# Choosing experts for both token tiles at once, both tiles' transposes ahead of the logits, and three forget-gate matmuls five steps later

## The chip, the core and the metric

The kernel runs on one core of a Trainium2 chip. The metric is the device time of one execution in microseconds. PE is the matrix engine, PEld its weight loads, DVE the vector engine, ACT the scalar engine, POOL GpSimd, and SP the engine whose queue issues nearly all loads of weights. A term used throughout: an engine takes its own instructions in the order in which they stand in its queue, so an instruction that waits holds up those behind it.

## What is computed

A decoder trunk of two layers on 256 tokens of width 1024, all in float32. Layer 0 mixes with a state-space scan (S5). Then one shared set of keys, values and forget gates is made, and layer 1 mixes with attention that reads it. Each layer ends in a mixture of 32 experts: a router picks one group of 8 experts out of 4 by the largest group logit, then the two best experts of that group. Cut to the two places that matter here:

```
def shared_kv(x, ...):                  # after layer 0
    k, v, fz = split(h @ kv_w)          # fz: (256, 16)
    logf = log_sigmoid(fz + kv_fb)
    fcum = cumsum(logf, over tokens)    # enters the attention logits of layer 1

def hier_moe(h, ...):                   # in both layers
    g_logits = t @ wg + bg              # (256, 4)
    g_top_v, g_idx = top_k(g_logits, 1)
    e_logits = (t @ we + be).reshape(-1, 4, 8)
    e_sel = e_logits at group g_idx
    top_v, top_i = top_k(e_sel, 2)
    w = softmax(top_v) * softmax(g_logits) at g_idx
    out = sum over the chosen experts of  w * (silu(t @ w1) * (t @ w3)) @ w2
```

## The kernel before

Tokens lie on the 128 partitions, as two tiles (i = 0, 1). All weights stream from HBM in blocks of 1 MB into a ring of 12 slots, to which the expert stages add some (`grow`). SP issues the loads in program order (`fetch`, L71), and a load waits until the work that last read its slot is done. So the stream runs at full rate while slots come free fast enough, and stands still while they don't.

**Order of work.** A scheduler places the instructions of ACT, DVE and POOL by its own model of time. Two stretches are written by hand: the start of each layer's experts (`start`, L571) on all engines, and PE's order alone from the keys and values to the end of the attention layer (`in_order`).

**The experts.** `start` finishes the last half of the residual stream `h`, transposes it on PE (`across`, L328; result copied to `hT` by ACT for tile 0 and by DVE for tile 1), forms the logits with 4 small matmuls for each tile and half (`logits`, L358), and takes the root mean square on DVE and POOL (`norm`, L341, result `rstds`). `step(fill, 4)` then puts 16 matmuls of a later gate on PE (L188). They read four weight blocks of the ring, which is how those four slots come free; ahead of them POOL clears a tile `rows` (L183) and SP loads two small bias rows into it (L185). Next come the choice of experts (`route_tile`, DVE alone), five small matmuls that count tokens per expert (`weigh`, L398), the placing matrix (`place`, L430), the gathering of tokens (`gather`, L441: PE, then ACT and DVE) and the first expert weights (`first`, L479), whose matmuls (L486) free the next slots. The loads of expert weights are put on SP's queue by `load`, at the end of `start` in program order.

`route_tile` is a generator for one tile. The two are run in lockstep, so that DVE gets step 1 of tile 0, step 1 of tile 1, step 2 of tile 0, and so on: 16 steps, 32 instructions, each step working on at most 36 columns.

**Keys, values and forget gates.** `project` (L1156) multiplies by a 512-column half of a weight matrix in eight steps ("quarters" of a block). For each quarter ACT and DVE split the weights into two parts (`split_next`, L1104 and L1105, three buffers `ws`), and PE does six matmuls of 512 columns (L1162). After each quarter, `tick` (L1117) advances a list of side jobs by one step. One of them is `forget_gates` (L1199): matmuls, a transpose, then a long chain of small DVE instructions for log-sigmoid that ends in `f_z` (L1239), then three small matmuls that sum over tokens:

```
V.scalar_tensor_tensor(fz, fp, -2.0, fz, op0=OP.mult, op1=OP.add)     # L1239
yield
pc = mm_tile()
PE.matmul(pc[:, 0:16], tri, fz[:, 0:16], start=True, stop=True)       # L1242
```

and two DVE copies of the sums (L1245, L1246). The job starts while the second half of the keys is projected and ends after the second quarter of the values (`project(hk, 0, use_v)`, L1409).

Of the kernel before, what the change touches and what calls it, by code (L numbers as in the profile page):

```python
# [15 lines left out]
OP = mybir.AluOpType  # L16
AX = mybir.AxisListType.X
# [5 lines left out]
NE = 32  # L23
# [4 lines left out]
BIG = 1e30  # L28
# [11 lines left out]
def trunk(ctx: ExitStack, tc: tile.TileContext, A, out, ring=12, ring2=4, ring3=5, ring4=3, ring5=4, lpb=2, TK=2):  # L40
    nc = tc.nc
    V, S, G, PE = nc.vector, nc.scalar, nc.gpsimd, nc.tensor
# [15 lines left out]
    def mm_tile():  # L58
        return psum.tile([128, 512], F32, tag="mm", name="mm", bufs=4)
# [56 lines left out]
    desc = const.tile([128, NE], F32, name="desc")  # L116
# [108 lines left out]
    def square(ssq, i, n):  # L225
        S.activation(mm_tile(), h[:, i, 512 * n:512 * n + 512], AF.Square, accum_out=ssq[:, i, n:n + 1])
# [85 lines left out]
    def moe(l, sh, g, gbc, c36, slots_):  # L312
# [13 lines left out]
        rstd = ma.tile([128, 2], F32, name="rstds")  # L326
# [25 lines left out]
        gm, gs, m1, m2, top, e2, r1, w1 = (t2(n, 1) for n in ("gm", "gs", "m1", "m2", "top", "e2", "r1", "w1"))  # L352
# [3 lines left out]
        pls = []  # L356

        def logits(i, n):  # L358
            if not pls:
                pls.append(acc_tile())  # L360
            for k in range(4 * n, 4 * n + 4):
                PE.matmul(pls[0][:, 64 * i:64 * i + 36], hTs[i][:, k, :], sw[:, k],
                          start=k == 0 and i == 0, stop=k == KD - 1, skip_group_check=True)

        def route_tile(pl, i):

            V.scalar_tensor_tensor(lg[:, i], pl[:, 64 * i:64 * i + 36], rstd[:, i:i + 1], c36, op0=OP.mult, op1=OP.add)
            yield
            gl = lg[:, i, 0:4]

            def rank_first(x, w, mx):

                V.tensor_reduce(mx[:, i], x, axis=AX, op=OP.max)
                yield
                V.scalar_tensor_tensor(cand[:, i, 0:w], x, mx[:, i], desc[:, NE - w:], op0=OP.is_equal, op1=OP.mult)
                yield
                V.tensor_reduce(top[:, i], cand[:, i, 0:w], axis=AX, op=OP.max)
                yield

            yield from rank_first(gl, 4, gm)  # L380
            V.tensor_scalar(gc[:, i], cand[:, i, 0:4], top[:, i], -BIG, op0=OP.is_lt, op1=OP.mult)
            yield
            V.tensor_tensor(ml[:, i].rearrange("p (a b) -> p a b", b=8),
                            lg[:, i, 4:36].rearrange("p (a b) -> p a b", b=8),
                            gc[:, i, :, None].to_broadcast([128, 4, 8]), op=OP.add)
            yield
            yield from rank_first(ml[:, i], NE, m1)
            V.tensor_scalar(o1[:, i], cand[:, i], top[:, i], None, op0=OP.is_equal)
            yield
            V.scalar_tensor_tensor(ml2[:, i], o1[:, i], -BIG, ml[:, i], op0=OP.mult, op1=OP.add)  # L390
            yield
            yield from rank_first(ml2[:, i], NE, m2)
            V.tensor_scalar(o2[:, i], cand[:, i], top[:, i], None, op0=OP.is_equal)
            yield
            V.tensor_tensor(selb[:, i], o1[:, i], o2[:, i], op=OP.add)
            yield

        def weigh():  # L398

# [171 lines left out]
        def start(gated, ssq, fill, after):  # L571

            with tc.manual_schedule(engines=ENGINES):
                steps = [gated(i) for i in range(2)]
                for st in steps:
                    next(st)
                for i, st in enumerate(steps):
                    next(st)
                    across(i, 1)
                    square(ssq, i, 1)  # L580
                    logits(i, 1)
                after()
                mb.append(es.enter_context(tc.tile_pool(name=f"moeb{l}", bufs=1, side="right")))
                norm(ssq)
                step(fill, 4)
                for _ in zip(*[route_tile(pls[0], i) for i in range(2)]):
                    pass
                mosti = weigh()
                place(0)
                gather(0)  # L590
                gate_values()
            load(l)
            return mosti
# [605 lines left out]
    def forget_gates():  # L1199


        pz = mm_tile()
        for kh in range(2):
            for a in range(2):
                for q in range(4):
                    k = 4 * kh + q
                    PE.matmul(pz[32 * q:32 * q + 32, :T], smallw[:, k, 0:32], hk[:, k, a, :].bitcast(F32),
                              start=kh + a == 0, stop=kh + a == 2)
        z4 = tp.tile([128, T], F32, tag="xf", name="z4", bufs=2)
        S.activation(z4, pz[:, :T], AF.Copy)  # L1210
        yield
        pt = mm_tile()
        for i in range(2):
            PE.transpose(pt[:, 128 * i:128 * i + 128], z4[:, 128 * i:128 * i + 128], ident)

        def a32(n):
            return ap.tile(t32, F32, name="f_" + n)

        fz, fa, fe, fs, f2, fp = (a32(n) for n in ("z", "a", "e", "s", "2", "p"))
        V.tensor_reduce(fz.rearrange("p (i e) -> p i e", i=2),  # L1220
                        pt[:, :T].rearrange("p (i q e) -> p i e q", i=2, q=4)[:, :, 0:16, :], axis=AX, op=OP.add)
        V.tensor_tensor(fz, fz, cols[:, C_FBR:C_FBR + 32], op=OP.add)
        V.tensor_scalar(fa, fz, -1.0, None, op0=OP.mult)
        V.tensor_tensor(fa, fa, fz, op=OP.min)
        yield
        p, two = exp_parts(ap, fa, t32)
        yield
        V.tensor_tensor(fe, p, two, op=OP.add)
        V.tensor_scalar(fs, fe, 2.0, None, op0=OP.add)
        V.reciprocal(fs, fs)  # L1230
        V.tensor_tensor(fs, fs, fe, op=OP.mult)
        V.tensor_tensor(f2, fs, fs, op=OP.mult)
        V.tensor_scalar(fp, f2, 1.0 / 15, None, op0=OP.mult)
        yield
        for c in (13, 11, 9, 7, 5, 3):
            V.scalar_tensor_tensor(fp, fp, 1.0 / c, f2, op0=OP.add, op1=OP.mult)
        V.scalar_tensor_tensor(fp, fp, 1.0, fs, op0=OP.add, op1=OP.mult)
        V.tensor_scalar(fz, fz, 0.0, None, op0=OP.min)
        V.scalar_tensor_tensor(fz, fp, -2.0, fz, op0=OP.mult, op1=OP.add)  # L1239
        yield  # L1240
        pc = mm_tile()
        PE.matmul(pc[:, 0:16], tri, fz[:, 0:16], start=True, stop=True)  # L1242
        PE.matmul(pc[:, 16:32], ones, fz[:, 0:16], start=True, stop=False)
        PE.matmul(pc[:, 16:32], tri, fz[:, 16:32], start=False, stop=True)
        V.tensor_copy(qn[:, :, :, 65], pc[:, :32].rearrange("p (i a) -> p i a", i=2))  # L1245
        V.tensor_scalar(kn[:, :, :, 64], pc[:, :32].rearrange("p (i a) -> p i a", i=2), -1.0, None, op0=OP.mult)  # L1246
# [335 lines left out]
```

## Time and profile before

| what | value |
|---|---|
| median of 3 runs | 818.82 us (817.67 to 820.29) |
| the profiled execution | 819.66 us, of which the span from the first to the last instruction is 817.9 us |
| mean granted clock of PE | 0.945 of full speed |
| PE / DVE / ACT / POOL busy | 86% / 47% / 28% / 6% of the span |
| moved from and to HBM | 299.30 MB, mean 366 GB/s over the span |

A busy share is an average over stages with different limits: in both layers' experts the DMA engines run at about 425 GB/s and set the pace; between them PE does. A row "idle before <- releaser" gives the idle time of that engine just before the instruction and what ended it. The granted clock is 1.00 at 2.4 GHz and 0.50 at 1.2 GHz.

### The profile page before, as it was taken

The numbers are of one execution on the slowest core, as the hardware profiler recorded it, in microseconds if no ns is written. First come the engines' busy times: TensorE is split into PE (matmuls) and PEld (weight loads), VectorE is DVE, ScalarE is ACT, GpSimd is POOL, SyncE is SP. The second block draws the span as 40 slices with busy tenths as digits, with TensorE's granted clock in tenths as the row PEclk, the third lists the DMA queues.
The fourth block names the chain that finished last, engine by engine and source line by source line (L and its number), as shares of the span: only waits on it lengthen the run. The fifth ranks groups of instructions, "written<-read, shape, count | busy, mean of one in ns | idle before, by whom it ended". The sixth has DMA issues, their size and how long they took to land. (4 is left out here: it accounts for less than half of the span.)

```text
span 817.9 us, 13668 instructions
## 1 busy us (share of the span) xinstructions
PE 706.3 (86%) x5510; PEld 402.8 (49%) x5510; DVE 381.3 (47%) x1025; ACT 232.1 (28%) x537; POOL 46.7 (6%) x52
## 2 busy tenths in 40 slices
PE   2797999898899998786779899999988999986776
PEld 0674776575533533131157567888764333331311
DVE  7685999774322332111165655775554222221202
ACT  4423333162201110000043265878722101100100
POOL 2000000000000000000001101570000000000000
PEclk9899999998999999789679999999999999999888
DMA  9998946777999999999999857592989999999996
GB/s 368 426 425 347 406 150 250 292 314 277 426 426 426 426 425 425 428 423 427 424 424 426 315 197 312 204 370 98 349 347 415 426 428 424 427 427 427 425 426 260
DMA packets 41828, 299.30 MB, mean 366 GB/s; under 512 B 4632, under 2 KB 4760, under 8 KB 5664
## 3 DMA queue, kind: packets, MB, share of 16 engines
q1 hardware_dynamic: 41344, 297.14, 88.3%
q10 hardware_dynamic: 416, 1.23, 0.4%
q8 instruction: 45, 0.74, 0.3%
q14 instruction: 23, 0.19, 0.1%
HBM read 297.31 MB, written 1.05 MB: 365 GB/s over the span
## 5 line engine op out<-in xcount | busy, mean ns | idle before, releaser
L486 PE MATMUL mm<-w,xg 128*32 128x512 f32 x1024 | 141.4, 637 | 24.0 <-DMA w<-wa 10.7
L486 PEld LDWEIGHTS mm<-w,xg 128*32 128x32 f32 x1024 | 29.6, 111 | 110.6 <-issue 62.8
L458 ACT ACTIVATE xg<-mm,sh,g 128x128 f32<-128x128 f32 x64 | 29.3, 457 | 181.0 <-PE mm L450 164.8
L1105 DVE TENSOR_TENSOR ws<-w,ws 128x512 fp32r<-128x512 f32 x80 | 58.2, 733 | 40.4 <-ACT ws L1104 40.1
L501 PE MATMUL mm<-w,aT 128*32 128x512 f32 x512 | 68.3, 655 | 9.2 <-DMA w<-wb 3.6
L450 PE MATMUL mm<-Pr,h 128*128 128x128 f32 x512 | 65.3, 281 | 11.2 <-DVE Pr L438 11.2
L1162 PE MATMUL acc<-ws,hn 128*128 128x512 f32 x288 | 73.9, 415 | 0.6 <-ACT hn L1140 0.6
L450 PEld LDWEIGHTS mm<-Pr,h 128*128 128x128 f32 x512 | 60.9, 194 | 26.6 <-issue 19.0
L508 PE MATMUL acc<-y,Sc 128*128 128x512 f32 x128 | 64.7, 629 | 6.5 <-DVE y L504 6.5
L1104 ACT ACTIVATE ws<-w 128x512 fp32r<-128x512 f32 x80 | 49.9, 629 | 54.5 <-PE acc L1162 43.6
L1162 PEld LDWEIGHTS acc<-ws,hn 128*128 128x128 f32 x288 | 56.0, 197 | 16.7 <-ACT hn L1140 1.9
L456 DVE TENSOR_SCALAR xg<-mm,g,sh 128x128 f32<-128x128 f32 x64 | 26.2, 410 | 74.1 <-ACT xg L458 74.1
L504 DVE TENSOR_TENSOR y<-mm,gbc 128x512 f32<-128x512 f32 x32 | 22.1, 692 | 64.7 <-PE mm L501 64.5
L491 ACT ACTIVATE a<-mm 128x256 f32<-128x256 f32 x16 | 6.1, 383 | 161.2 <-PE mm L486 161.2
L469 DVE COPY Sc<-mm 128x256 f32<-128x256 f32 x16 | 6.8, 425 | 83.8 <-PE mm L467 83.8
L508 PEld LDWEIGHTS acc<-y,Sc 128*128 128x128 f32 x128 | 22.2, 193 | 45.6 <-issue 26.8
L492 DVE TENSOR_TENSOR a<-a,mm 128x256 f32<-128x256 f32 x16 | 6.7, 419 | 75.0 <-ACT a L491 75.0
L501 PEld LDWEIGHTS mm<-w,aT 128*32 128x32 f32 x512 | 14.4, 114 | 50.6 <-issue 34.4
L785 PE MATMUL mm<-hnT,w 128*64 128x128 f32 x512 | 33.1, 289 | 2.7 <-ACT hnT L255 2.7
L961 PE MATMUL acc<-w,uT 128*128 128x512 f32 x64 | 30.5, 621 | 5.6 <-ACT uT L950 5.5
L785 PEld LDWEIGHTS mm<-hnT,w 128*64 128x64 f32 x512 | 31.3, 143 | 4.4 <-ACT hnT L255 3.7
L173 PE MATMUL mm<-w,sc 128*32 128x256 f32 x512 | 29.2, 380 | 0.0
(327 smaller groups left out, 951.8 us busy)
## 6 DMA issues: line engine op xcount, KB each, us to landing
w<-wa SPq DMA_DIRECT2D x128, 1024.0 KB, 19.5
w<-wb SPq DMA_DIRECT2D x64, 1024.0 KB, 19.7
w<-ada SPq DMA_DIRECT2D x36, 1024.0 KB, 10.6
w<-ada00s SPq DMA_DIRECT2D x8, 1024.0 KB, 18.1
w<-kvada SPq DMA_DIRECT2D x8, 1024.0 KB, 9.0
w<-win SPq DMA_DIRECT2D x4, 1024.0 KB, 14.9
w<-ada00g SPq DMA_DIRECT2D x4, 1024.0 KB, 18.8
w<-woutv SPq DMA_DIRECT2D x4, 1024.0 KB, 17.2
```

The lines of the kernel that those rows point to most:

```text
L173: PE.matmul(ps[32 * q:32 * q + 32, 0:256], sc32(2 * b + kk), bands(w[:, 1024 * kk:1024 * kk + 1024])[:, q], start=b + kk == 0, stop=b == 3 ...
L450: PE.matmul(px[:, 128 * c4:128 * c4 + 128], h[:, i, 128 * c:128 * c + 128], Pr[:, i].rearrange("p a b -> p (a b)"), start=i == 0, stop=i == 1)
L456: V.tensor_scalar(xg[:, c], src, g[:, c:c + 1], sh[:, c:c + 1], op0=OP.mult, op1=OP.add)
L458: S.activation(xg[:, c], src, AF.Identity, bias=sh[:, c:c + 1], scale=g[:, c:c + 1])
L486: PE.matmul(ph[32 * s:32 * s + 32, :], xg[:, k, 32 * s:32 * s + 32], w[:, 512 * s:512 * s + 512], start=k == 0, stop=k == KD - 1)
L501: PE.matmul(py[32 * s:32 * s + 32, :], aT[:, 128 * f + 32 * s:128 * f + 32 * s + 32], w[:, 512 * s:512 * s + 512], start=f == 0, stop=f == 1)
L508: PE.matmul(acc[i][n], scs[q][:, 128 * i:128 * i + 128], y[:, 512 * n:512 * n + 512], start=q == 0, stop=q == NQ - 1, skip_group_check=True)
L785: PE.matmul(ps[64 * v:64 * v + 64, 128 * hh:128 * hh + 128], w[:, k, c0:c0 + 64], hnT[:, k, v::2], start=k == 0 and hh == 0, stop=k == KD ...
L961: PE.matmul(val[t][n], uT[:, m, 128 * t:128 * t + 128], wval[m // 2][:, c0:c0 + 512], start=m == 0, stop=m == 7)
L1104: S.activation(o[:, 0], w, AF.Copy)
L1105: V.tensor_tensor(o[:, 1], w, o[:, 0].bitcast(F32), op=OP.subtract)
L1162: PE.matmul(pk[i], src[:, k, a, 128 * i:128 * i + 128], w[:, b], start=k + a + b == 0, stop=k == KD - 1 and b == 1)
```

## The change

Three edits.

1. In `start`, the transposes of both tiles are put on PE before the logits of either.
2. `route` takes the place of the two `route_tile` generators: one chain of instructions that work on both tiles side by side (up to 64 columns). What was one instruction with a scalar per token ("equal to the maximum, times rank") becomes two tensor instructions with a broadcast operand. 32 instructions become 21; only the logits and the masking of groups are still done for each tile.
3. `forget_gates` lets five more steps of `tick` go by before it asks PE for the three sums.

```diff
@@ -362,38 +362,32 @@
                 PE.matmul(pls[0][:, 64 * i:64 * i + 36], hTs[i][:, k, :], sw[:, k],
                           start=k == 0 and i == 0, stop=k == KD - 1, skip_group_check=True)
 
-        def route_tile(pl, i):
-
-            V.scalar_tensor_tensor(lg[:, i], pl[:, 64 * i:64 * i + 36], rstd[:, i:i + 1], c36, op0=OP.mult, op1=OP.add)
-            yield
-            gl = lg[:, i, 0:4]
+        def route(pl):
+
+            for i in range(2):
+                V.scalar_tensor_tensor(lg[:, i], pl[:, 64 * i:64 * i + 36], rstd[:, i:i + 1], c36,
+                                       op0=OP.mult, op1=OP.add)
 
             def rank_first(x, w, mx):
 
-                V.tensor_reduce(mx[:, i], x, axis=AX, op=OP.max)
-                yield
-                V.scalar_tensor_tensor(cand[:, i, 0:w], x, mx[:, i], desc[:, NE - w:], op0=OP.is_equal, op1=OP.mult)
-                yield
-                V.tensor_reduce(top[:, i], cand[:, i, 0:w], axis=AX, op=OP.max)
-                yield
-
-            yield from rank_first(gl, 4, gm)
-            V.tensor_scalar(gc[:, i], cand[:, i, 0:4], top[:, i], -BIG, op0=OP.is_lt, op1=OP.mult)
-            yield
-            V.tensor_tensor(ml[:, i].rearrange("p (a b) -> p a b", b=8),
-                            lg[:, i, 4:36].rearrange("p (a b) -> p a b", b=8),
-                            gc[:, i, :, None].to_broadcast([128, 4, 8]), op=OP.add)
-            yield
-            yield from rank_first(ml[:, i], NE, m1)
-            V.tensor_scalar(o1[:, i], cand[:, i], top[:, i], None, op0=OP.is_equal)
-            yield
-            V.scalar_tensor_tensor(ml2[:, i], o1[:, i], -BIG, ml[:, i], op0=OP.mult, op1=OP.add)
-            yield
-            yield from rank_first(ml2[:, i], NE, m2)
-            V.tensor_scalar(o2[:, i], cand[:, i], top[:, i], None, op0=OP.is_equal)
-            yield
-            V.tensor_tensor(selb[:, i], o1[:, i], o2[:, i], op=OP.add)
-            yield
+                V.tensor_reduce(mx[:, :, 0], x, axis=AX, op=OP.max)
+                V.tensor_tensor(cand[:, :, 0:w], x, mx.to_broadcast([128, 2, w]), op=OP.is_equal)
+                V.tensor_tensor(cand[:, :, 0:w], cand[:, :, 0:w],
+                                desc[:, None, NE - w:].to_broadcast([128, 2, w]), op=OP.mult)
+                V.tensor_reduce(top[:, :, 0], cand[:, :, 0:w], axis=AX, op=OP.max)
+
+            rank_first(lg[:, :, 0:4], 4, gm)
+            V.tensor_tensor(gc, cand[:, :, 0:4], top.to_broadcast([128, 2, 4]), op=OP.is_lt)
+            for i in range(2):
+                V.scalar_tensor_tensor(ml[:, i].rearrange("p (a b) -> p a b", b=8),
+                                       gc[:, i, :, None].to_broadcast([128, 4, 8]), -BIG,
+                                       lg[:, i, 4:36].rearrange("p (a b) -> p a b", b=8), op0=OP.mult, op1=OP.add)
+            rank_first(ml, NE, m1)
+            V.tensor_tensor(o1, cand, top.to_broadcast([128, 2, NE]), op=OP.is_equal)
+            V.scalar_tensor_tensor(ml2, o1, -BIG, ml, op0=OP.mult, op1=OP.add)
+            rank_first(ml2, NE, m2)
+            V.tensor_tensor(o2, cand, top.to_broadcast([128, 2, NE]), op=OP.is_equal)
+            V.tensor_tensor(selb, o1, o2, op=OP.add)
 
         def weigh():
 
@@ -578,13 +572,13 @@
                     next(st)
                     across(i, 1)
                     square(ssq, i, 1)
+                for i in range(2):
                     logits(i, 1)
                 after()
                 mb.append(es.enter_context(tc.tile_pool(name=f"moeb{l}", bufs=1, side="right")))
                 norm(ssq)
                 step(fill, 4)
-                for _ in zip(*[route_tile(pls[0], i) for i in range(2)]):
-                    pass
+                route(pls[0])
                 mosti = weigh()
                 place(0)
                 gather(0)
@@ -1238,6 +1232,8 @@
         V.tensor_scalar(fz, fz, 0.0, None, op0=OP.min)
         V.scalar_tensor_tensor(fz, fp, -2.0, fz, op0=OP.mult, op1=OP.add)
         yield
+        for _ in range(5):
+            yield
         pc = mm_tile()
         PE.matmul(pc[:, 0:16], tri, fz[:, 0:16], start=True, stop=True)
         PE.matmul(pc[:, 16:32], ones, fz[:, 0:16], start=True, stop=False)
```

Where instructions stand on the engines, before and after. Line numbers after the change are lower by 6 in `start` and by 4 or 6 further down.

PE at the forget gates. L1162 (L1156 after) are the projections of keys and values, six matmuls to a quarter; the rows with `f_z` are the three sums; L173 is a modulation matmul; L1129 the transposes for the queries. Before:

```order
L173 MATMUL mm<-w,sc 32x256 x32
L1162 MATMUL acc<-ws,hn 128x512 x12
L1242 MATMUL mm<-f_z,tri 128x16
L1243 MATMUL mm<-f_z,ones 128x16
L1244 MATMUL mm<-f_z,tri 128x16
L1162 MATMUL acc<-ws,hn 128x512 x84
```

After:

```order
L173 MATMUL mm<-w,sc 32x256 x32
L1156 MATMUL acc<-ws,hn 128x512 x42
L1238 MATMUL mm<-f_z,tri 128x16
L1239 MATMUL mm<-f_z,ones 128x16
L1240 MATMUL mm<-f_z,tri 128x16
L1156 MATMUL acc<-ws,hn 128x512 x54
```

The three sums now stand behind 42 projection matmuls instead of 12: seven quarters instead of two, out of the same 96.

DVE at the same place. `ws` is the DVE half of splitting one quarter of weights; `f_s`, `f_p` and `f_z` belong to the forget gates' chain, and L1245 and L1246 copy the sums out. Before:

```order
L1231 TENSOR_TENSOR f_s<-f_s,f_e 128x32
L1232 TENSOR_TENSOR f_3782<-f_s 128x32
L1233 TENSOR_SCALAR f_p<-f_3782 128x32
L1236 SCALAR_TENSOR_TENSOR f_p<-f_p,f_3782 128x32 x6
L1237 SCALAR_TENSOR_TENSOR f_p<-f_p,f_s 128x32
L1239 SCALAR_TENSOR_TENSOR f_z<-f_p,f_z 128x32
L1245 COPY qn<-mm 128x32
L1246 TENSOR_SCALAR kn<-mm 128x32
L1105 TENSOR_TENSOR ws<-w,ws 128x512 x14
```

After:

```order
L1225 TENSOR_TENSOR f_s<-f_s,f_e 128x32
L1226 TENSOR_TENSOR f_3771<-f_s 128x32
L1227 TENSOR_SCALAR f_p<-f_3771 128x32
L1099 TENSOR_TENSOR ws<-w,ws 128x512
L1230 SCALAR_TENSOR_TENSOR f_p<-f_p,f_3771 128x32 x3
L1099 TENSOR_TENSOR ws<-w,ws 128x512
L1230 SCALAR_TENSOR_TENSOR f_p<-f_p,f_3771 128x32 x3
L1099 TENSOR_TENSOR ws<-w,ws 128x512
L1231 SCALAR_TENSOR_TENSOR f_p<-f_p,f_s 128x32
L1233 SCALAR_TENSOR_TENSOR f_z<-f_p,f_z 128x32
L1099 TENSOR_TENSOR ws<-w,ws 128x512
L1241 COPY qn<-mm 128x32
```

Four quarters of weights are now split between the chain's steps and ahead of the copies that wait for PE; before, the chain and the copies stood in one piece. On ACT, POOL and SP nothing stands elsewhere.

PE at the start of layer 1's experts. L333 are transposes (4 for a tile and half), L362 logits (4 for a tile and half), L1399 (L1395 after) the last output projection, L188 the gate's matmuls. Before:

```order
L1399 MATMUL acc<-ws,oT 128x512 x4
L333 MATMUL mm<-ident,h 128x128 x8
L362 MATMUL acc<-smallw,hT 128x36 x12
L333 MATMUL mm<-ident,h 128x128 x4
L362 MATMUL acc<-smallw,hT 128x36 x4
L188 MATMUL acc<-w,sc 32x512 x16
```

After:

```order
L1395 MATMUL acc<-ws,oT 128x512 x4
L333 MATMUL mm<-ident,h 128x128 x8
L362 MATMUL acc<-smallw,hT 128x36 x4
L333 MATMUL mm<-ident,h 128x128 x4
L362 MATMUL acc<-smallw,hT 128x36 x12
L188 MATMUL acc<-w,sc 32x512 x16
```

The last transposes, those of tile 1, move from behind 12 logit matmuls to behind 4, and the last logits follow the others without a transpose in between. In layer 0 the same edit turns transposes, logits, transposes, logits (4 each) into 8 transposes and 8 logits.

## Rows read from the trace of the kernel before

**Rows 1.** The page: GB/s moved in 40 equal slices of 20.4 us.
```profile
GB/s 368 426 425 347 406 150 250 292 314 277 426 426 426 426 425 425 428 423 427 424 424 426 315 197 312 204 370 98 349 347 415 426 428 424 427 427 427 425 426 260
```

**Rows 2.** The chain that ended last, in order of time: start, us, what.
```profile
792.41 7.14 DMA w<-wa
```

**Rows 3.** Stretches (us): busy us of each engine, granted clock, DMA share, GB/s.
```profile
196.00:416.00 220.00, 183.36 (x1174) 71.95 (x1175) 57.06 (x185) 25.07 (x57) 2.76 (x6) 0.91 1.01 426
416.00:456.00 40.00, 39.32 (x279) 28.23 (x278) 25.66 (x63) 17.12 (x30) 6.77 (x6) 0.89 0.99 413
```

**Rows 4.** Timeline at the forget gates: start us, us, engine, line, instruction, idle before it.
```profile
456.70 0.69 DVE L1105 TENSOR_TENSOR ws<-w,ws 128x512 fp32r<-128x512 f32 x1
457.13 0.63 ACT L1104 ACTIVATE ws<-w 128x512 fp32r<-128x512 f32 x1 [0.77 <-PE acc L1162]
...
459.07 1.32 DVE L1236 SCALAR_TENSOR_TENSOR f_p<-f_p,f 128x32 f32<-128x32 f32 x6
...
460.99 0.37 PE L1242 MATMUL mm<-f_z,tri 128*128 128x16 f32 x2 [3.89 <-DVE f_z L1239]
...
461.65 20.69 PE L1162 MATMUL acc<-ws,hn 128*128 128x512 f32 x81
...
464.33 0.63 ACT L1104 ACTIVATE ws<-w 128x512 fp32r<-128x512 f32 x1 [6.56 <-PE acc L1162]
...
466.28 0.63 ACT L1104 ACTIVATE ws<-w 128x512 fp32r<-128x512 f32 x1 [1.32 <-PE acc L1162]
...
467.68 0.63 ACT L1104 ACTIVATE ws<-w 128x512 fp32r<-128x512 f32 x1 [0.77 <-PE acc L1162]
```

**Rows 5.** Stretches of half a microsecond after PE's wait for the forget gates.
```profile
461.50:462.00 0.50, 0.50 (x5) 0.46 (x5) 0.16 (x2) 0.00 (x0) 0.00 (x0) 0.96 1.08 459
462.00:462.50 0.50, 0.50 (x3) 0.40 (x2) 0.15 (x2) 0.00 (x0) 0.00 (x0) 0.50 1.00 426
...
465.00:465.50 0.50, 0.50 (x3) 0.40 (x2) 0.50 (x1) 0.00 (x0) 0.00 (x0) 0.62 0.85 360
```

**Rows 6.** PE's waits from 463 to 606 us, longest first: total us, times, longest.
```profile
PE mm L188 <- DVE xf L1136: 0.9, 1, 0.9
...
PE acc L1399 <- DVE oT L1391: 0.2, 1, 0.2
```

**Rows 7.** Timeline of the start of layer 1's experts, all engines.
```profile
603.30 1.08 PE L362 MATMUL acc<-smallw,hT 128*128 128x36 f32 x8 [0.78 <-DVE hT L337]
...
604.31 3.64 PE L188 MATMUL acc<-w,sc 128*32 128x512 f32 x32
...
604.50 0.42 DVE L367 SCALAR_TENSOR_TENSOR lg<-acc,rstds,c 128x36 f32<-128x36 f32 x2 [0.92 <-POOL rstds L345]
...
608.33 0.32 DVE L395 TENSOR_TENSOR selb<-o,o 128x32 bf16<-128x32 f32 x2
...
608.96 0.23 DVE L410 SCALAR_TENSOR_TENSOR rk<-mm,selb 128x64 f32<-128x64 f32 x1 [0.17 <-PE mm L409]
```

**Rows 8.** Timeline of SP's queue there: when each group of loads is issued.
```profile
604.92 0.54 SPq L185 DMA_DIRECT2D rows<-gbias  x2
605.56 2.78 SPq L71 DMA_DIRECT2D w<-wa  x4
...
615.24 0.33 SPq L71 DMA_DIRECT2D w<-wa  x1
```

**Rows 9.** Stretches of 2 us there.
```profile
604.00:606.00 2.00, 2.00 (x20) 0.81 (x23) 1.50 (x13) 0.00 (x0) 0.90 (x2) 1.00 0.00 1
...
616.00:618.00 2.00, 2.00 (x24) 0.52 (x16) 1.82 (x11) 0.92 (x1) 0.00 (x0) 1.00 0.99 336
```

**Rows 10.** Instructions by tile: count, ns min/median/max, first and last start, shape.
```profile
L395 DVE TENSOR_TENSOR selb<-o,o x4: 184/189/193, 202.0 to 608.5; 128x32 bf16<-128x32 f32 x4
...
L373 DVE TENSOR_REDUCE m<-ml x8: 179/183/188, 199.6 to 607.4; 128x1 f32<-128x32 f32 x8
...
L436 DVE TENSOR_TENSOR P<-slot,rk x32: 280/282/285, 204.5 to 759.9; 128x128 f32<-128x128 f32 x32
```

## The prediction

> **What bounds the kernel now.** I read the rate of the transfers first, then the end of the chain, then each stage's waits. In the slices of the span [rows 1] the stream of weights runs at about 425 GB/s in two long stretches, slices 11 to 22 and 31 to 39. Those are the experts of the two layers. From 196 to 416 us the DMA engines are busy for a share of 1.01 [rows 3]: layer 0's experts, routing included, lie entirely under the stream. The chain that ended last begins with a load of expert weights [rows 2], so layer 1's end is set by when its stream starts and how many bytes it has.
>
> Between the two stretches the stream is slower, because slots come free only as PE gets through them. From 463 to 606 us PE waits four times, 2.2 us in all, and for no load [rows 6]. So what PE saves between 416 and 606 us should move all that follows. What is saved in layer 0's routing should be lost under the stream.
>
> At the start of layer 1's experts the stream stands still: nothing is moved from 604 to 606 us [rows 9]. Two things restart it [rows 8]. At 605.56 four loads begin to go out: they stand behind the bias rows, which wait for POOL, and their slots come from the gate's matmuls (L188). The next load follows only at 615.24, when the first expert weights have been used, and it comes a little late: 616 to 618 us moves 336 GB/s instead of 425, a loss of 2 x 89/425 = 0.4 us [rows 9]. So the second trigger, at the end of routing and gathering, is the one that counts, and it counts closely.
>
> **Forget gates.** PE stands idle for 3.89 us in front of the sums, until DVE has `f_z` [rows 4]. Then PE's clock, which was 1.00, falls to 0.50 from 462 to about 465.3 us [rows 5]. What this costs is seen from ACT, which starts a split whenever PE has finished a quarter [rows 4]. At full clock quarters are 467.68 - 466.28 = 1.40 us apart. The first quarter after the sums takes from 461.65 to 464.33, 2.65 without the signal's delay, and the second 1.95. That is 1.25 + 0.55 = 1.80 us lost to the clock.
>
> After the change five more quarters stand ahead of the sums. Is there work for PE? Three buffers hold split weights, so the third quarter is ready when PE ends the second at 457.10. A freed buffer is filled after 0.63 us on ACT and 0.69 on DVE [rows 4], within 1.40. DVE has 0.68 us of chain between two splits (three steps of 0.226), so 1.37 us of work per 1.40. Stepping through the new order: PE ends the sixth quarter at 462.7 and the seventh at 464.1; DVE splits the eighth's weights (freed at 458.5 + 1.4 a quarter) from 462.0, then does the last two steps, and `f_z` is there at about 463.2. The sums find it 0.9 us early, and the clock has no gap to fall in. The copies behind the sums hold up the split of the tenth quarter by 0.5 us, which is needed 2 us later. The sums' own 0.65 us is still paid. Gain: 3.89 + 1.80 = **5.7 us**. Were `f_z` later than the sums' turn, PE would wait for just the difference. The bounds are 3.9 (the clock falls all the same) and 5.7.
>
> **Transposes first.** In layer 0 the stream covers it; without that cover it would be worth about 0.8 us, PE's wait for `hT`. In layer 1 PE waits 0.78 us for the copy of tile 1 before the last logits [rows 7]. Now the other logits run during that copy, so they end at about 603.5 instead of 604.38. `rstds` on POOL, which follows the same copy on DVE, comes earlier by more. So the logits' first step on DVE starts at 603.6 instead of 604.50: **0.9 us**. Clearing of `rows`, the bias loads and L188 move up as well, and with them the first four loads, by some 0.85 us.
>
> **The choice of experts.** Before, 4.15 us pass from 604.50 to the end of `selb` at 608.65 [rows 7]. With 32 instructions this is 0.13 us each, though one lasts 0.189 [rows 10]: the two tiles' steps overlap, as the pair `selb` shows, 0.32 us for both [rows 7]. After the change nearly every instruction waits for the one just ahead of it. Six such dependent steps of 32 columns take 1.32 us [rows 4], (1.32 - 0.19)/5 = 0.226 from start to start, that is the duration and 0.037. Durations grow by (282 - 189)/96 = 0.97 ns per column [rows 10], which makes 0.220 for 64 columns, 0.214 for a reduction and 0.166 for 8. The new chain: logits 0.45; five steps on 8 columns at 0.20, 1.0; the masking pair 0.36; eight steps at 0.257 and four reductions at 0.251, 3.06; less the last gap, 4.83. With PE's five counting matmuls, the first of which used to start on tile 0 alone, `rk` comes **0.7 us later** after the logits.
>
> No row shows these shapes, so both ends: at 0.13 per instruction 21 take 2.7 us (1.4 less than now); with 64 columns as dear as 128, 0.282, the chain takes 5.6 (1.5 more). I take 4.8, since dependent steps in this same kernel follow that pitch.
>
> The Trainium skill ("VectorE: DVE Perf Modes", Rules for kernel authors) advises the fewest operations in a chain, because a flush follows each one. By that rule 21 for 32 would be 1.4 us gained; the trace doesn't agree where two tiles alternate, since a pair takes 0.32 and not 0.38 us.
>
> Net in layer 1: 0.9 - 0.7 = **0.2 us** earlier for the second trigger. In layer 0, nothing.
>
> **The sum.** 5.7 + 0.2 = 5.9 us. The profiled execution took 819.66, so 813.8 by its own time. The median of the runs is 0.84 lower, at 818.82, which makes **812.9 us**.
>
> **Rivals.**
> - *Only the wait goes* (11%). The clock falls there all the same, or `f_z` is short of time for part of it, its slack being 0.9 us. Then 3.9 + 0.2: 814.7.
> - *Instructions count, not their dependence* (6%). The choice takes 2.7 us. Triggers come 0.85 us earlier and the late 0.4 can be won back, more can't: 5.7 + 1.3, 811.8. Against it: the dependent steps in [rows 4].
> - *The clock falls at layer 1's gap* (11%, and 2% together with the first: 816.5). L188 now ends at 607.1 and the counting matmuls start at 608.4, an idle 1.3 us where 0.62 was, followed by the same 1.2 before the gathering. A low stretch like the one in [rows 5] costs 1.8: 814.7. For it: a wait did that in [rows 5]; against it: that wait was three times as long.
> - *The lead is swallowed* (7%). Some load between 463 and 606 us sets its own pace and PE waits for it. Then routing's 0.2 alone: 818.6, no change that can be measured. Against it: PE waits for no load there [rows 6], and several slices move less than 320 GB/s [rows 1].
> - *PE becomes layer 1's bound* (3%), the one that ends slower. After the gap the clock stays low through the experts. PE is busy for 183 of 220 us in layer 0 [rows 3], 17% to spare; at 0.50 it does about half, so each low microsecond loses 0.5, of which 0.17 was spare: some 0.3. It decides against the change from (5.9 + 2.5)/0.3 = 28 us in one piece; with 40 it would be 825. Against it: the mean clock of 0.91 in layer 0 means some 40 us at 0.50, and the stream stayed full.
>
> **How the numbers follow.** A measurement here tells about 0.3%, 2.5 us, from no change. The forecast has 60%. Faster are it and the rivals at 814.7, 811.8 and 814.7: 60 + 11 + 6 + 11 = 88%. Same are the swallowed lead and the double case, 9%; slower 3%. The range from 811.0 to 816.5 holds all that ends faster and the double case, with room for the spread of the runs (817.67 to 820.29).
>
> **What the new profile would show.** PE's sums with no idle time ahead of them and a clock of 1.00 throughout 456 to 468 us; from there on PE's work 5.7 us earlier. In layer 1: no wait for `hT` before the last logits; 4.8 us (not 2.7, not 4.15) from the logits' step to `selb`; the stream's pause starts 5.7 us and ends 6.5 us earlier, and the load after the first four goes out 5.9 us earlier; layer 0's stream is unchanged to 416 us. I am wrong if PE waits elsewhere between 457 and 600 us, above all for a load, or if the gap at 607 us costs clock.

## The result and the profile after

The changed kernel takes 813.34 us (median of 6 runs, 811.29 to 814.84) against 819.3 for the kernel before beside it (817.45 to 820.29). The ratio is 0.9935, with an interval from 0.9918 to 0.9951. A second comparison, with more runs of the kernel before, gave 812.68 against 818.56 us and 0.9929 (0.9911 to 0.9946). So some 5.9 us are gained. The profiled execution took 814.26 us, with a span of 812.5.

**Forget gates.** PE's timeline in the kernel before, for the stretch by which this document measures that place: from the first quarter of the values to the transposes for the queries, 482.88 - 454.03 = 28.85 us.

```profile
454.03 3.06 PE L1162 MATMUL acc<-ws,hn 128*128 128x512 f32 x12
...
482.88 1.36 PE L1129 MATMUL mm<-ident,xs 128*128 128x128 f32 x11
```

The same stretch after the change, timeline of all engines, to be held against [rows 4]:

```profile
451.52 10.07 PE L1156 MATMUL acc<-ws,hn 128*128 128x512 f32 x42
...
460.32 0.19 DVE L1233 SCALAR_TENSOR_TENSOR f_z<-f_p,f_z 128x32 f32<-128x32 f32 x1
...
461.43 0.29 PE L1238 MATMUL mm<-f_z,tri 128*128 128x16 f32 x2
...
462.01 12.84 PE L1156 MATMUL acc<-ws,hn 128*128 128x512 f32 x54
...
474.69 0.49 PE L1123 MATMUL mm<-ident,xs 128*128 128x128 f32 x3
```

The sums have no idle time in front of them: `f_z` is done at 460.51, 0.92 us before their turn. The stretch takes 474.69 - 451.52 = 23.17 us, 5.68 less. Stretches of the span, beside [rows 3]:

```profile
196.00:416.00 220.00, 181.05 (x1177) 70.59 (x1177) 57.40 (x172) 25.39 (x58) 2.60 (x6) 0.93 1.01 425
416.00:456.00 40.00, 39.38 (x282) 28.29 (x281) 27.38 (x70) 17.77 (x31) 7.02 (x5) 0.93 1.01 426
456.00:468.00 12.00, 12.00 (x56) 9.76 (x56) 7.46 (x21) 6.12 (x11) 0.00 (x0) 1.00 0.97 394
```

From 456 to 468 us PE is busy throughout at a granted clock of 1.00 (2.4 GHz). Layer 0's stream is as full as before. PE's waits from there to layer 1's counting matmuls, beside [rows 6]:

```profile
PE mm L399 <- DVE selb L390: 1.4, 1, 1.4
PE mm L188 <- DVE xf L1130: 0.9, 1, 0.9
PE mm L1310 <- ACT pr L1296: 0.3, 1, 0.3
PE acc L1395 <- DVE oT L1387: 0.2, 1, 0.2
```

No load stands among them, and the wait for `hT` is gone. At the top there is a new one, for the choice of experts.

**Start of layer 1's experts.** Timeline, beside [rows 7]. Before:

```profile
599.21 2.84 PE L362 MATMUL acc<-smallw,hT 128*128 128x36 f32 x24
...
610.14 4.04 PE L450 MATMUL mm<-Pr,h 128*128 128x128 f32 x32 [1.22 <-DVE Pr L438]
...
614.12 7.07 PE L486 MATMUL mm<-w,xg 128*32 128x512 f32 x64
```

After:

```profile
591.07 1.05 PE L362 MATMUL acc<-smallw,hT 128*128 128x36 f32 x8
...
592.42 2.77 PE L362 MATMUL acc<-smallw,hT 128*128 128x36 f32 x24
...
595.12 3.64 PE L188 MATMUL acc<-w,sc 128*32 128x512 f32 x32
...
595.31 0.42 DVE L368 SCALAR_TENSOR_TENSOR lg<-acc,rstds,c 128x36 f32<-128x36 f32 x2 [1.65 <-PE acc L362]
...
597.34 0.22 DVE L374 TENSOR_TENSOR cand<-ml,m 128x64 f32<-128x64 f32 x1
...
599.91 0.22 DVE L390 TENSOR_TENSOR selb<-o,o 128x64 bf16<-128x64 f32 x1
...
600.20 0.19 PE L399 MATMUL mm<-selb,trib 128*128 128x32 bf16 x1 [1.44 <-DVE selb L390]
...
601.70 5.67 PE L444 MATMUL mm<-Pr,h 128*128 128x128 f32 x32 [1.22 <-DVE Pr L432]
...
607.30 7.07 PE L480 MATMUL mm<-w,xg 128*32 128x512 f32 x64
```

From the logits' step to the end of `selb` it is 600.13 - 595.31 = 4.82 us (4.15 before); the chain's last steps, of 64 columns and each waiting for the one ahead, start 0.26 us apart, ten times over from 597.34 to 599.91. PE stands idle for 1.44 us ahead of the counting matmuls and for 1.22 us ahead of the gathering, and the gathering takes 5.67 us. In the kernel before it took 4.04. From the first logits to the first expert weights it is 614.12 - 599.21 = 14.91 us before and 607.30 - 591.07 = 16.23 after. SP's queue, beside [rows 8]:

```profile
596.25 12.52 SPq L71 DMA_DIRECT2D w<-wa  x5
```

Stretches of 2 us there, beside [rows 9] (the last three numbers are granted clock, DMA share and GB/s):

```profile
602.00:604.00 2.00, 2.00 (x11) 1.87 (x10) 0.08 (x1) 0.00 (x0) 0.00 (x0) 0.60 1.00 422
604.00:606.00 2.00, 2.00 (x12) 2.00 (x12) 0.13 (x1) 0.46 (x1) 0.00 (x0) 0.55 1.04 434
...
608.00:610.00 2.00, 2.00 (x24) 0.61 (x20) 1.37 (x7) 1.63 (x2) 0.00 (x0) 1.00 0.44 78
```

The first four loads go out at 596.25, 9.3 us earlier. The fifth is the last of its group, which ends at 608.77 and whose single issues last 0.33, so it starts at about 608.4, only 6.8 us earlier. In between the stream runs dry: 78 GB/s from 608 to 610 us, where the late load before cost a stretch of 336 [rows 9]. The two rows above it show why: during the gathering the clock is 0.60 and 0.55.

One thing here is not the change's. The values start at 451.52 instead of 454.03: PE was already 2.5 us ahead before it reached the forget gates, and the only edit ahead of them, in layer 0's experts, lies under the stream. The experiments had to say how much such leads differ between executions.

### The profile page after: what moved, and what is told of

The parts are those of the page before. It is cut to its first block, busy times and chain, and to the rows that moved or that the text cites. A ratio compares the mean times of both kernels' runs of the same rounds, so it can differ in the third digit from the quotient of the medians.

```text
span 812.5 us, 13647 instructions
## 1 busy us (share of the span) xinstructions
PE 704.3 (87%) x5510; PEld 402.9 (50%) x5510; DVE 379.2 (47%) x1003; ACT 232.1 (29%) x537; POOL 46.8 (6%) x52
## 3 DMA queue, kind: packets, MB, share of 16 engines
HBM read 297.31 MB, written 1.05 MB: 367 GB/s over the span
## 5 line engine op out<-in xcount | busy, mean ns | idle before, releaser
L444 PE MATMUL mm<-Pr,h 128*128 128x128 f32 x512 | 67.8, 289 | 11.2 <-DVE Pr L432 11.2
L444 PEld LDWEIGHTS mm<-Pr,h 128*128 128x128 f32 x512 | 63.4, 202 | 24.8 <-issue 18.9
L1156 PE MATMUL acc<-ws,hn 128*128 128x512 f32 x288 | 72.0, 407 | 0.6 <-ACT hn L1134 0.6
L1156 PEld LDWEIGHTS acc<-ws,hn 128*128 128x128 f32 x288 | 54.5, 192 | 16.2 <-ACT hn L1134 1.9
L173 PE MATMUL mm<-w,sc 128*32 128x256 f32 x512 | 29.2, 380 | 0.0
```

What stands on the lines that cost most here:

```text
L173: PE.matmul(ps[32 * q:32 * q + 32, 0:256], sc32(2 * b + kk), bands(w[:, 1024 * kk:1024 * kk + 1024])[:, q], start=b + kk == 0, stop=b == 3 ...
L444: PE.matmul(px[:, 128 * c4:128 * c4 + 128], h[:, i, 128 * c:128 * c + 128], Pr[:, i].rearrange("p a b -> p (a b)"), start=i == 0, stop=i == 1)
L1156: PE.matmul(pk[i], src[:, k, a, 128 * i:128 * i + 128], w[:, b], start=k + a + b == 0, stop=k == KD - 1 and b == 1)
```

## The experiments

The kernel before, run beside them on the same chip, took 818.11 us in the median (24 runs) for experiments 1 to 4, 818.56 (23) for 5 to 8, and 818.45 (17) for 9 to 12.

**1. The forget gates alone.**

```diff
         V.scalar_tensor_tensor(fz, fp, -2.0, fz, op0=OP.mult, op1=OP.add)
         yield
+        for _ in range(5):
+            yield
         pc = mm_tile()
```

> Only the five steps of the forget gates, routing as before. If the lead is the wait plus the clock (3.9 + 1.8), this kernel is 5.7 us below the one before and has no idle time ahead of the three sums. If only the wait counts, 3.9 us. If part of the changed kernel's lead comes from the routing, as the 2.5 us by which PE was ahead at the first quarter of the values already might say, this kernel gets less than 4 us.

Measured: 813.23 us, ratio 0.9935 (0.9912 to 0.9958). The stretch from values to queries takes 23.17 us, as in the full change. So this edit has the whole gain that a measurement can tell. But at layer 1's start, where nothing was edited, PE's timeline now reads:

```profile
593.50 1.89 PE L362 MATMUL acc<-smallw,hT 128*128 128x36 f32 x8 [0.78 <-DVE hT L337]
595.32 6.13 PE L188 MATMUL acc<-w,sc 128*32 128x512 f32 x32
601.38 0.19 PE L405 MATMUL mm<-selb,trib 128*128 128x32 bf16 x1
```

The last logits take 1.89 us instead of 1.08 and the gate's matmuls 6.13 instead of 3.64 [rows 7]. The counting matmuls wait for PE here and not for DVE.

**2. The routing alone** (both edits in `start`, without the five steps).

```diff
-        for _ in range(5):
-            yield
```

> Only the two routing edits, forget gates as before. By the sum of the prediction the second trigger comes 0.2 us earlier (no change in the time); with the fallen clock seen in the changed kernel's gathering it comes 1.4 us later, so 0.2 us faster to 1.4 us slower. If the number of instructions decided, 1.3 us faster. If the routing in layer 0 gives the 2.5 us lead, 2.5 us faster.

Measured: 817.21 us, ratio 0.9989 (0.9973 to 1.0006): no change that can be told. PE waits 3.89 us for `f_z` as before. PE at layer 1's start:

```profile
606.28 0.19 PE L399 MATMUL mm<-selb,trib 128*128 128x32 bf16 x1 [1.43 <-DVE selb L390]
...
607.78 4.04 PE L444 MATMUL mm<-Pr,h 128*128 128x128 f32 x32 [1.21 <-DVE Pr L432]
```

The same idle time of 1.43 us stands there, the choice takes the same 4.82 us, and yet the gathering runs at full clock. From the first logits to the first expert weights it is 14.60 us, where the kernel before has 14.91: the routing's own worth is 0.3 us when the clock holds.

**3. The transposes alone.**

```diff
                     across(i, 1)
                     square(ssq, i, 1)
+                for i in range(2):
                     logits(i, 1)
```

> Only the transposes ahead of the logits, choice of experts in lockstep as before. By the working of the prediction the logits' first step and with it the counting of tokens come 0.9 us earlier against the first transposes of layer 1, the choice takes 4.15 us as before, and the time falls by at most 0.9 us, within noise. If the order on PE does nothing by itself, nothing moves.

Measured: 816.84 us, ratio 0.9986 (0.9969 to 1.0003), no change that can be told. The choice of experts, old here, takes 4.14 us. The low clock behind the 3.89 us of waiting lasted longer in its profile (values to queries 30.44 us), and the gate's matmuls took 5.01 us.

**4. Forget gates and transposes, with the old choice of experts** (experiments 1 and 3 together).

> The changed kernel with the choice of experts of before. If the chain on both tiles is the slower one and its gap lets PE's clock fall, this kernel is 0.7 to 2.3 us below the changed kernel (813.3), gathers in 4.0 us at a clock of 1.00 and is about 6.6 us below the one before. If fewer instructions were a gain, it is 1.3 us above the changed kernel.

Measured: 812.04 us, ratio 0.9926 (0.9903 to 0.9949). Values to queries 23.16 us; first logits to first expert weights 13.85 us, 1.06 less than before, with the clock at 1.00. The new choice of experts, all that the full change has beyond this, brings nothing that can be told: the two intervals overlap almost whole.

**5. Two steps instead of five.**

```diff
-        for _ in range(5):
+        for _ in range(2):
             yield
```

> The change with two steps of tick in place of five ahead of the three sums: they stand behind four quarters of projection instead of seven (and of two before). Theory (PE waits for just the time by which f_z is late): PE comes to the sums 2.8 us later than in the kernel before and f_z is held up by two more splits of weights on DVE, so that about 2.5 us of idle time stay ahead of the sums. If the clock falls behind that idle time as it did behind 3.89 us, the stretch from the first quarter of the values to the transposes for the queries takes about 27.4 us (before 28.85, change 23.17) and the program 4 us longer than the change; if it holds, 25.6 us, and 2.5 us longer than the change. Rival (the order alone pays, the number of quarters doesn't matter): 23.2 us and the time of the change.

Measured: 815.85 us, ratio 0.9968 (0.9954 to 0.9983), 3.2 us above the change. PE:

```profile
461.85 0.58 PE L1238 MATMUL mm<-f_z,tri 128*128 128x16 f32 x2 [2.54 <-DVE f_z L1233]
...
463.12 19.32 PE L1156 MATMUL acc<-ws,hn 128*128 128x512 f32 x72
482.28 1.91 PE L1123 MATMUL mm<-ident,xs 128*128 128x128 f32 x16
```

The wait is 2.54 us, the worked-out 2.5. PE waits for just the difference, so the number of steps matters. Behind it the clock falls for longer: even the sums take 0.58 us each instead of 0.37, and values to queries is 28.83 us (27.4 expected). Of that 23.17 is work and 2.54 the wait, so 3.1 us went to the clock.

**6. The change with its gap filled.** Three matmuls, whose result nothing reads, stand in the idle time ahead of the counting matmuls.

```diff
                 step(fill, 4)
+                pj = mm_tile()
+                for _ in range(3):
+                    PE.matmul(pj[:, 0:224], ident, h[:, 0, 0:224], start=True, stop=True)
                 route(pls[0])
```

> The change with three matmuls of 224 columns, some 1.2 us, put on PE between the gate's matmuls and the matmuls that count tokens; they read the residual stream and nothing reads their result, so only work is added. Theory A (the longer idle time of 1.44 us ahead of the counting matmuls is what made the clock fall in the change's profile): with the gap filled the gathering takes 4.04 us at a clock of 1.00 instead of 5.67, and the median is about 1.5 us below the change. Theory B (where the clock falls at layer 1's start differs from execution to execution): the median is that of the change, within 0.3 us, and the profile may show a fall at that place or not.

Measured: 810.48 us, ratio 0.9900 (0.9884 to 0.9916), 2.2 us below the change beside it (experiment 8) and the lowest median here. PE's timeline:

```profile
598.41 1.40 PE L583 MATMUL mm<-h,ident 128*128 128x224 f32 x6
599.92 0.19 PE L399 MATMUL mm<-selb,trib 128*128 128x32 bf16 x1
...
601.43 4.05 PE L444 MATMUL mm<-Pr,h 128*128 128x128 f32 x32 [1.22 <-DVE Pr L432]
605.40 7.07 PE L480 MATMUL mm<-w,xg 128*32 128x512 f32 x64
```

More work, less time: the gathering takes 4.05 us, and the fifth load of SP's group goes out 1.9 us earlier than in the change's second profile (experiment 8). This rests on five runs and one profile, and the interval overlaps a little with that of experiment 8 (0.9911 to 0.9946).

**7. The wait filled in the kernel before.** Four matmuls that nothing reads stand ahead of the sums.

```diff
         yield
+        pj = mm_tile()
+        for _ in range(4):
+            PE.matmul(pj, ident, h[:, 0, 0:512], start=True, stop=True)
         pc = mm_tile()
```

> The kernel before with four matmuls of 512 columns in float32, some 3.5 us, put on PE directly ahead of the three sums; they read activations that are long there and nothing reads their result, so only work is added. PE is busy where it waited 3.89 us for f_z. Theory (the clock fell because PE stood idle): idle ahead of the sums below 0.5 us, the clock at 1.00 from 456 to 468 us, the two quarters behind the sums 1.40 us each, the stretch from the first quarter of the values to the transposes for the queries about 27.0 us instead of 28.85, and the median 1.8 us below the kernel before. Rival (the fall comes of something else at that place, the sums or DVE's work): the clock falls all the same, 28.8 us, and the median is that of the kernel before or above.

Measured: 818.17 us, ratio 0.9993 (0.9976 to 1.0010). PE:

```profile
452.69 3.60 PE L1243 MATMUL mm<-h,ident 128*128 128x512 f32 x8
456.74 0.37 PE L1245 MATMUL mm<-f_z,tri 128*128 128x16 f32 x2 [0.46 <-DVE f_z L1239]
...
597.57 1.92 PE L362 MATMUL acc<-smallw,hT 128*128 128x36 f32 x8 [0.78 <-DVE hT L337]
599.42 5.79 PE L188 MATMUL acc<-w,sc 128*32 128x512 f32 x32
```

The fall behind the sums is gone: clock 1.00 from 456 to 477 us, values to queries 27.31 us, which is the 23.17 of work and the filled wait. The fall stands in all six profiles here that have an unfilled wait ahead of the sums (three of the kernel before, experiments 2, 3 and 5), and in neither of the two with it filled (this and experiment 12). So idleness did make the clock fall there. But the median doesn't show the 1.8 us, though its interval just reaches that far. In this profile, as in experiment 1, the clock falls at layer 1's start instead.

**8. The change again.**

> The change once more, for a second profile of the same program. If the fall of the clock at the gathering in layer 1 belongs to the program (the longer gap ahead of the counting matmuls), it stands there again: gathering 5.7 us. If it belongs to the execution: gathering 4.0 us, the first expert weights 1.6 us earlier after the logits. Either way no idle time ahead of the three sums and 23.2 us from the first quarter of the values to the transposes for the queries. Time 813.3 us, ratio to the kernel before 0.993.

Measured: 812.68 us, as told above; span 810.6, values to queries 23.16, and the low clock at the same place:

```profile
600.18 0.19 PE L399 MATMUL mm<-selb,trib 128*128 128x32 bf16 x1 [1.44 <-DVE selb L390]
...
601.69 5.67 PE L444 MATMUL mm<-Pr,h 128*128 128x128 f32 x32 [1.22 <-DVE Pr L432]
```

The loss of 1.63 us stands in both profiles of the change, and not in that with the gap filled. The theory that the execution decides is not excluded by this: experiments 2 and 5 have the same gap and no loss.

**9 and 10. The kernel before, twice more.**

> The kernel before once more, for a second profile. Theory (where the clock falls outside the forget gates differs between executions): the 3.89 us of idle time and the fall behind it stand again, 28 to 30.5 us from the first quarter of the values to the transposes for the queries; from the first logits of layer 1 to the first expert weights either 14.9 us, as in the first profile, or some 17 us with the gate's matmuls at the low clock, as in the kernels with the gates alone and with the wait filled. If it takes 14.9 again, that stretch is the kernel's own, and the loss of 2.2 us there in the kernel with the filled wait came with the edit.

> The kernel before a third time, expected as the second: the same wait and fall at the forget gates, and at layer 1's start either 14.9 us or some 17 us from the first logits to the first expert weights.

Single runs of 820.31 and 819.10 us. PE in the first of them:

```profile
411.22 1.06 PE L1129 MATMUL mm<-ident,xs 128*128 128x128 f32 x8 [3.34 <-DMA w<-wk]
...
456.56 0.37 PE L1242 MATMUL mm<-f_z,tri 128*128 128x16 f32 x2 [3.89 <-DVE f_z L1239]
...
480.02 1.91 PE L1129 MATMUL mm<-ident,xs 128*128 128x128 f32 x16
...
602.31 5.96 PE L188 MATMUL acc<-w,sc 128*32 128x512 f32 x32
```

The same program shows both patterns. In this execution the keys' transposes start at 411.22 us, the clock behind the wait is low for longer (values to queries 30.41 us), and at layer 1's start the gate's matmuls take 5.96 us. In the other one they start at 414.21 us, and the rest is as in the first profile: 28.85 and 14.90 us. The spans are nearly equal, 818.5 and 817.3.

**11. Experiment 4 with its gap filled** (one matmul of 320 columns, read by nothing).

```diff
                 step(fill, 4)
+                pj = mm_tile()
+                PE.matmul(pj[:, 0:320], ident, h[:, 0, 0:320], start=True, stop=True)
                 for _ in zip(*[route_tile(pls[0], i) for i in range(2)]):
```

> The kernel with the five steps and the transposes first, with the old choice of experts, and one matmul of 320 columns (some 0.56 us) that nothing reads in the 0.62 us ahead of the counting matmuls. Theory A (the old choice of experts is 0.68 us shorter and a filled gap keeps the clock): about 0.7 us below the change with its gap filled, near 809.8 us. Theory B (0.62 us of idle time costs no clock in most executions): the time of the same kernel without the filling, 812.0 us.

Measured: 811.32 us, ratio 0.9904 (0.9888 to 0.9920). By the interval it can be told neither from experiment 4 nor from 6. PE had no idle time ahead of the gate's matmuls, and still, in stretches of 2 us:

```profile
592.00:594.00 2.00, 2.00 (x19) 1.96 (x19) 0.43 (x3) 0.00 (x0) 1.17 (x2) 1.00 1.03 434
594.00:596.00 2.00, 2.00 (x13) 0.59 (x16) 1.81 (x15) 0.00 (x0) 0.00 (x0) 0.54 0.17 68
```

**12. The wait filled and the transposes first.**

> The kernel before with the 3.89 us of waiting filled by four matmuls that nothing reads, and the transposes first. Theory (with the wait filled the clock fell instead at layer 1's start, behind the 0.78 us that PE waits for the copy of tile 1; without that wait it holds): 27.3 us from the first quarter of the values to the transposes for the queries, the gate's matmuls of layer 1 at 1.00 (3.64 us), and 1.5 for the clock and 0.9 for the transposes, 2.4 us below the kernel before. Rival (the low stretch comes at layer 1's start whatever stands there): at most 1 us below the kernel before.

Measured: 816.30 us, ratio 0.9977 (0.9963 to 0.9991), 1.9 us by the ratio where 2.4 was expected. Values to queries 27.30 us, but the gate's matmuls take 5.00 us: the clock fell at layer 1's start though the 0.78 us of waiting was gone. The reason given for experiment 7's loss, that wait, is therefore not enough. The loss is smaller, though: 14.74 us from the first logits to the first expert weights are 0.9 more than in experiment 4, where experiment 7 lost 2.2.

**All profiles side by side**, in us: when the keys' transposes start; values to queries; first logits of layer 1 to its first expert weights; from there to the end of the span.

| profile | keys | values to queries | start of layer 1 | rest |
|---|---|---|---|---|
| before, first / third | 415.08 / 414.21 | 28.85 / 28.85 | 14.91 / 14.90 | 203.8 / 204.0 |
| before, second | 411.22 | 30.41 | 17.32 | 204.8 |
| change, first / second | 412.93 / 412.96 | 23.17 / 23.16 | 16.23 / 16.24 | 205.2 / 203.3 |
| 1, gates | 411.56 | 23.17 | 17.46 | 203.9 |
| 2, routing | 413.32 | 28.87 | 14.60 | 203.4 |
| 3, transposes | 412.10 | 30.44 | 14.74 | 205.6 |
| 4, gates and transposes | 414.16 | 23.16 | 13.85 | 203.8 |
| 5, two steps | 414.50 | 28.83 | 14.61 | 203.8 |
| 6, filled gap | 412.71 | 23.15 | 14.61 | 203.3 |
| 7, filled wait | 411.38 | 27.31 | 17.14 | 203.7 |
| 11, gates, transposes, filled | 411.45 | 23.16 | 15.43 | 204.7 |
| 12, filled wait, transposes | 412.03 | 27.30 | 14.74 | 204.7 |

Where the keys start at 413.3 or later, the clock held at layer 1's start (five profiles). Where they start earlier, it fell there in eight profiles of nine, all but that of experiment 6. The loss behind the 3.89 us of waiting goes the same way: 1.8 us in the three profiles with a late start of the keys, 3.4 in the two with an early one; experiment 5, with a late start, lost 3.1 behind a shorter wait. The division at 413.3 was found after the fact, and no run shows what ties the places, 180 us apart.

## Why the prediction was right, and where its steps were not

**The bound** held. PE's lead is carried whole: from the transposes for the queries to layer 1's first logits it is 116.33 us before and 116.38 after, and PE waits for no load. Layer 0's stream didn't notice its routing.

**Forget gates, 5.7 us**: 5.68 in the profile. `f_z` came 0.92 us early (0.9 worked out), and experiment 5 shows the wait to be just the difference. Of its two parts the wait, 3.89, is as sure as a row can be. The clock's 1.80 was mis-sized: the step read it from one profile, and other profiles of the same wait lost 1.8, 3.35 (second of before, 30.41 - 23.17 - 3.89) and 3.4 us (experiment 3). What that part brings in the median by itself stays open: experiment 7 removed the fall and gained nothing that can be told.

**Transposes first, 0.9 us**: from [rows 7] the logits' step moved by 604.50 - 595.31 = 9.19, of which 8.14 came with the first logits (599.21 to 591.07). The edit is worth 1.05. Experiment 4 has the same 1.06, from the first logits to the first expert weights.

**The choice of experts, 4.83 us**: 4.82. The pitch of dependent steps decided, and not the count of instructions: where the clock held, the start of layer 1 takes 14.60 us with the new choice (experiment 2) and 13.85 with the old (experiment 4), so this edit by itself costs some 0.75 us. By the rule of the Trainium skill ("VectorE: DVE Perf Modes", Rules for kernel authors), 21 for 32 should have been shorter; the measurement says 0.67 us longer, since two independent tiles had covered each other's waits.

**The net of 0.2 us for the second trigger** was 0.3 where the clock held (experiments 2, 5 and 6). In the change's own profiles it failed as the rival with 11% had it: the clock falls behind layer 1's gap, which the prediction had named as a sign that it was wrong. "That wait was three times as long" spoke against it and was no protection. The gathering lost 1.63 us in both profiles (1.8 estimated). So layer 1's start as a whole lost 16.23 - 14.91 = 1.3 us against the first profile of before, where 0.2 was to be gained. Against the second, which has an early start of the keys as the change's profiles have, it gained 17.32 - 16.23 = 1.1. So it stays open how much of the loss is the longer gap's and how much the execution's. The load after the first four went out 6.8 us earlier, of which 2.5 is the earlier start of the values; the rest, 4.3, is 1.6 short of the 5.9 forecast.

**Why the time came out near the forecast all the same.** Against the first profile of before: 5.68 gained at the gates, 1.32 lost at layer 1's start, 1.4 lost behind it, and 2.5 gained by the earlier start of the values, together 5.4 = 817.9 - 812.5. Against the second: 7.24 and 1.09 gained, 1.9 lost by a later start of the values and 0.4 behind, together 6.0 = 818.5 - 812.5. What stands behind layer 1's start differs between the two profiles of the change as well, 205.2 and 203.3 us, and most of that is the clock again. The load that PE waits for last lands 192.5 and 192.3 us after the first expert weights, so the stream is not behind it. The matmuls after that load, in the first profile:

```profile
799.97 1.60 PE L495 MATMUL mm<-w,aT 128*32 128x512 f32 x8 [1.44 <-DMA w<-wb]
...
801.50 3.10 PE L502 MATMUL acc<-y,Sc 128*128 128x512 f32 x4
```

In the second profile they take 1.07 and 1.98 us, 1.65 less together.

The low clock's losses move between these places from execution to execution, in the kernel before too, and the sums differ little. The working took one profile's stretches for the kernel's own. Its sum of 5.9 is right, but not made up as it said: by its own terms and the lost 1.6 it would have been 4.3. That the time came so near was in part luck.

**The other rivals** did not come: no load set PE's pace, and layer 1's experts stayed bound by the stream up to its last load.

## What to carry to other kernels

Work that asks one engine for another's late result belongs as far down the asking engine's queue as its reader allows; what it gains is the wait, up to the slack, and this edit alone brought all of the change's gain that could be measured. Before merging two independent chains into one, compare their overlapped pitch (0.13 us here) with the dependent pitch of the merged shapes (0.26): fewer instructions took longer. And take a second profile before a stretch of low clock is put down to an edit: here the same program's stretches differ by 1.6 to 3.9 us.

## What was not expected of the hardware

- With 1.4 us of added matmuls that nothing reads the median came out 2.2 us lower (experiment 6, five runs), while 3.6 us of them in a longer wait gained nothing that can be told (experiment 7).
- An idle time of 1.4 us was followed by the low clock (1.2 GHz) in both profiles of the change, and not in experiment 2 or 5, with the same gap behind the same work.
- The clock also fell with no idle time of PE ahead of it: in experiment 11 from 1.00 to 0.54 between 594 and 596 us, where PE had been busy for 2.00 of the 2 us before, with matmuls of 36 columns and their weight loads.
